# A two-layer attention trunk on one core: layer A's second projection moved ahead of the compression

## The chip, the cores and the metric

The kernel runs on one core of one Trainium2 chip. The metric is the device time of one execution in microseconds (us), taken as the median of several runs. The engines are named as in the profile: PE is TensorE (matmuls, and transposes done as matmuls), DVE is VectorE, ACT is ScalarE, POOL is GpSimd and SP is SyncE, which here only starts transfers.

## The reference

The input is one sequence of 512 rows of 1024 values, and a memory of 256 rows. Layer A normalizes the rows, projects them once, and runs two attentions beside each other; their outputs go through one output projection and are added to the input. An MLP with squared ReLU follows. Then keys and values are computed once for layer B, whose attention, output projection and second MLP end the program. All is in 32-bit floats.

Layer A's main attention has 12 heads in three groups of four, each group with its own keys and values. Each head attends three ways: to compressed blocks of 32 rows, to the selected blocks (with 512 rows, all 8 blocks are among the 16 that may be selected), and to a sliding window of 512 rows. Cut to what matters:

```python
k_c = rope(rmsnorm(compress(split_heads(k_cmp, G), 0), k_norm[0]), cmp_end)
v_c = compress(split_heads(v_cmp, G), 1)
...
def compress(t, i):
    tb = (t[:, :, blk_tok] + cmp_pos[i]).reshape(B, G, n_cmp, CMP_BLOCK * D)
    return jax.nn.gelu(tb @ cmp_w1[i] + cmp_b1[i]) @ cmp_w2[i] + cmp_b2[i]
```

The three results are weighted by sigmoid gates and summed. The memory attention has four heads over the 256 memory rows.

## The kernel before, in words

Every product of two 32-bit matrices is made of three matmuls on PE (mm3, lines 250 to 255): each operand is split into a high and a low part, and high by high, high by low and low by high are summed. Weights come in by SP's queue (L241), ACT makes their high part (L246), and DVE or POOL the low one (L248). Rows are handled in four blocks of 128.

Layer A is written as generators, which yield after a few instructions, and a few drivers that decide who goes next. Its opening, at L733 to L765, goes so:

- proj_a(0) projects group 0: four queries' heads, the keys of the selected and window branch, and the values. In each of the four blocks, evac takes the sums from PSUM: ACT copies the values (L899), normf computes the norms (L493 to L508), DVE scales by the norm weights (L903, L904), rope rotates (L517 to L520), L700 scales by the norm, hilo splits (L659, L660), and later PE transposes the queries (L709) and the keys (L719), which ACT (L715, L666, L667) and DVE (L665) copy out. Rotation and L700 run on POOL, but for group 0's even blocks, which use DVE.
- Woven with it is a second projection, of w_a0: the raw keys and values for the compression and the gates, 420 columns wide, whose four blocks stay in four buffers of tag x.
- Then a queue of filler work is built (Work). First in it is the compression: hidden(0) and hidden(1) transpose the raw rows (L797), copy them into three buffers of tag x each (L803, L804), add positions on POOL (L817), split (L288, L291) and multiply by w_c1; finish makes the compressed keys and values. mem_kv(0), the memory's keys and values of layer A, is woven into it; its memory tiles are split at L269 (ACT) and L270 (DVE). Behind it stand proj_a(1), proj_a(2), mem_q, mem_keys, mem_kv(1) (the memory's keys and values for layer B) and the first half of the output projection, outpart(0, 4).

Then attend (L142) walks through the attention items: 16 of each of the three groups, with 4 for the compressed blocks among them, and 8 of the memory attention. An item's front computes scores (L996 and L997 for the first two row blocks, L1009 and L1010 for the others), the maximum (L1000, L1012), the exponential on ACT (L216) and the scaling of the probabilities on POOL (L684). Its back transposes them (L1039, L1045), evT copies them out on DVE or ACT (L690, L692), and PE multiplies by the values (L1058). The memory items have L619, L638 and L646 for these. After each front and each back, attend takes some steps from the queue, 2.0 a time in group 0, 1.16 in group 1, 1.46 in group 2 and 1.96 in the memory items. An item whose group isn't projected yet makes the queue run up to that name ("g1", "g2", "cmp", "mem").

That is the order in which the program is written. A scheduler then places the instructions of each engine with a simulated timeline, so the order on an engine differs from that of the source. Pools set limits on top: PSUM has 2 accumulator tiles (acc), 3 for scores (ps), 2 for transposes (pt) and 1 for outputs (po); in SBUF tag x has 8 buffers, the weights' tag w 4, and the rotated rows' tags tq and qki 2 each.

Of the kernel before, what the change touches and what calls it, by code (L numbers as in the profile page):

```python
# [68 lines left out]
def drain(*gens):  # L69
    for g in gens:  # L70
        for _ in g:
            pass


def chain(*gens):
    for g in gens:
        yield from g


def weave(main, fill, ratio):  # L80

    due, fill = 0.0, iter(fill)
    for _ in main:
        due += ratio
        while due >= 1.0:
            due -= 1.0
            if next(fill, END) is END:
                due = -1e9
        yield
    yield from fill  # L90
# [43 lines left out]
def paced(gen, n):  # L134

    while True:
        for _ in range(n):
            yield
        next(gen, None)
# [33 lines left out]
def spread(a, b, at, every):  # L173

    a = list(a)
    for i, x in enumerate(b):
        a.insert(at + i * (every + 1), x)
    return a


class K:
    def __init__(self, ctx, tc, ins, out):
# [12 lines left out]
        self.lab = "s"  # L195

    BUFS = dict(
        act=12, st=3, w=4, qk=8, pt4=4, p2=6, raw=2, tmp=4, sq=1, rb=1, tq=2, qki=2, ki=2, x=8, r1=1, r2=1, r3=1, r4=2, r5=2, r6=3, r7=2, nm=6, su=5, cr=6, c1=2, c2=2, nb=4,
        cs=2, stt=4, vcb=1, ab=1,
    )  # L200

# [523 lines left out]
    def layer_a(self):  # L725
        nc, ins = self.nc, self.ins
        xg = self.xg0
        ab = self.t("ab", [P, 768])
        gt = ab[:, 0:144].rearrange("p (b g) -> p b g", b=NB)
        KC = self.c("KC", [P, 3, 2, 32], F32R)  # L730
        vc = ab[0:96, 144:208]
        raw0, st = [], []

        def evac0(b, ps):
            t = self.t("x", [P, 420])
            nc.scalar.activation(t, ps, AF.Copy, scale=st[0][:, b : b + 1])
            raw0.append(t)
            ga = gt[:, b, :]
            nc.vector.tensor_scalar(out=ga, in0=t[:, 384:420], scalar1=-1.0, scalar2=80.0, op0=ALU.mult, op1=ALU.min)
            nc.scalar.activation(ga, ga, AF.Exp)  # L740
            nc.vector.tensor_scalar(out=ga, in0=ga, scalar1=1.0, scalar2=None, op0=ALU.add)
            nc.vector.reciprocal(out=ga, in_=ga)

        ga, kf, qm, kk, oT, om = [[] for _ in range(3)], [], [], [], [], []
        x0 = self.x

        def hook(k):
            if k + 1 < KT:
                self.xpart(k + 1)
            i = self.square(k, x0[k], nc.vector)  # L750
            if k == KT // 2:
                self.constants_in(i)
            if k == KT - 1:
                self.setup2()
                st.extend(self.stats_cols())
                self.ms = self.mem_stats()

        self.xpart(0)
        p0 = self.proj_a(
            0, xg, st, ga[0], banks=[self.pacc] * 2 + [self.pS] * 2, lo="v", fine=True, hook=hook  # L760
        )
        for _ in range(KT):
            next(p0)
        drain(weave(p0, self.proj(xg, ins["w_a0"], 420, evac0, lo="g", pool=[self.pS, self.pacc, self.pacc, self.pS]), RC[0]))
        e = st[1]  # L765
        hidden, finish = self.compress(raw0, KC, vc)
        cmp = dict(KC=KC, vc=vc)
        work, seen, self.kf1 = Work(), [], []
        comp = chain(hidden(0, self.pacc), weave(hidden(1, self.pacc), finish(0), RC[1]), finish(1))
        work.add(weave(comp, chain(self.mem_kv(0, kf)), RC[2]), "cmp")  # L770
        work.add(self.proj_a(1, xg, st, ga[1]), "g1")
        work.add(self.proj_a(2, xg, st, ga[2]), "g2", lambda: seen.count(0) == 20)
        work.add(self.mem_q(0, xg, ins["w_am"], e, qm), None, lambda: seen.count(1) == 20)
        work.add(self.mem_keys(0, kf, kk), "mem")
        work.add(self.mem_kv(1, self.kf1))
        work.add(self.outpart(oT, 0, 4, ins["w_ao"], ins["xT"], 0))
        L, C = zip(*[self.attn_a(g, ga[g], gt, cmp, oT) for g in range(3)])
        M = self.mem_items(kf, qm, kk, om, 3, "mem")
        items = spread(L[0], C[0], 8, 0) + spread(L[1], C[1], 1, 1) + spread(L[2], C[2], 1, 1) + M
        slow = Work()  # L780
        slow.add(paced(self.adds, PA), None, lambda: len(seen) >= 12)
        attend(items, work, slow, RA, seen)
        while work.step() is not END:
            pass
        drain(self.outpart(oT + om, 4, 8, ins["w_ao"], None, 4))
# [978 lines left out]
```

## Time and profile before

| | |
|---|---|
| median of 3 runs | 1319.93 us |
| the runs | 1315.16, 1319.93, 1320.21 us |
| span of the profiled execution | 1316.2 us |
| PE busy | 1266.8 us |
| DVE busy | 860.7 us |
| ACT busy | 772.2 us |
| POOL busy | 377.6 us |

The page lists for the profiled execution its span, from the first instruction to the last; its own time with what lies around the span is not listed apart. The span stands 3.7 us below the median of the runs, and 1.0 above the fastest of them. Layer A's attention ends about 353 us after the span's start; MLPs and layer B take the rest. Busy times overlap: the sum over the engines is far above the span.

### The profile page before, as it was taken

How to read it: one execution, taken by the hardware profiler on the slowest of the kernel's cores; microseconds unless marked ns; L12 is line 12 of the kernel's file. 1: busy time of each engine (PE TensorE's matmuls, PEld its weight loads, DVE VectorE, ACT ScalarE, POOL GpSimd, SP SyncE). 2: the span in 40 equal slices, each digit the busy share in tenths (PEclk: the TensorE clock that was granted, in tenths of full speed). 3: DMA queues.
4: the chain of work that ended last, by engine and by line, in shares of the span. 5: the costliest groups of instructions: out<-in, count | busy, mean ns of one | idle time of the engine just before them, and what ended most of it. 6: DMA issues, size and time to landing. Idle time of an engine off the chain costs nothing.

```text
span 1316.2 us, 18557 instructions
## 1 busy us (share of the span) xinstructions
PE 1266.8 (96%) x6468; PEld 1041.7 (79%) x6468; DVE 860.7 (65%) x1597; ACT 772.2 (59%) x1699; POOL 377.6 (29%) x478
## 2 busy tenths in 40 slices
PE   9789989999999999999999989989999999999998
PEld 7768777677688888888887888877768888888887
DVE  6987767744566656566588566675665655747566
ACT  6765668674575354453557457777657545354462
POOL 4455574443240000000003679562324000000000
PEclk9899989999999999999999999999999999999999
DMA  7333222334379697796965431210338879697434
GB/s 263 120 98 106 97 97 81 63 74 113 120 245 240 219 279 219 262 247 208 290 197 165 134 79 49 67 45 9 95 120 267 232 269 225 221 280 223 154 112 160
DMA packets 61837, 215.28 MB, mean 164 GB/s; under 512 B 6736, under 2 KB 14928, under 8 KB 61232
## 3 DMA queue, kind: packets, MB, share of 16 engines
q1 hardware_dynamic: 50800, 143.72, 32.9%
q0 software_dynamic: 9344, 35.77, 13.8%
q10 hardware_dynamic: 1600, 34.61, 7.2%
q8 instruction: 51, 0.84, 0.2%
q14 instruction: 42, 0.34, 0.1%
HBM read 208.83 MB, written 72.35 MB: 214 GB/s over the span
## 4 chain that ended last, share of the span: by engine, by line
PE 81%; DVE 8%; ACT 4%; issue 2%; POOL 2%; DMA 2%; POOLq 0%; ACTq 0%; DVEq 0%
PE s_ps L253 13%; PE s_ps L254 13%; PE s_ps L255 13%; PE s_acc L253 6%; PE s_acc L254 6%; PE s_acc L255 6%; PE s_pt L253 3%; PE s_pt L254 3%; PE s_pt L255 3%; PE s_po L1058 2%; DVE s_w L248 2%; PE s_ps L1500 1%; PE s_pt L1045 1%; ACT s_p L216 1%; PE s_ps L1009 1%
## 5 line engine op out<-in xcount | busy, mean ns | idle before, releaser
L248 DVE TENSOR_TENSOR s_w<-s_st,s_w 128x1024 fp32r<-128x1024 f32 (+3 forms) x240 | 290.1, 1213 | 260.3 <-ACT s_w L246 259.8
L246 ACT ACTIVATE s_w<-s_st 128x1024 fp32r<-128x1024 f32 (+4 forms) x272 | 263.8, 973 | 188.0 <-PE s_pt L255 49.5
L253 PE MATMUL s_ps<-s_act,s_w 128*128 128x512 f32 x568 | 222.6, 394 | 1.4 <-ACT s_act L288 1.4
L254 PE MATMUL s_ps<-s_act,s_w 128*128 128x512 f32 x568 | 222.0, 391 | 0.0
L255 PE MATMUL s_ps<-s_act,s_w 128*128 128x512 f32 x568 | 221.8, 391 | 0.0
L253 PEld LDWEIGHTS s_ps<-s_act,s_w 128*128 128x128 f32 x568 | 106.8, 188 | 26.1 <-ACT s_act L288 3.1
L254 PEld LDWEIGHTS s_ps<-s_act,s_w 128*128 128x128 f32 x568 | 106.9, 188 | 22.9 <-issue 0.8
L255 PEld LDWEIGHTS s_ps<-s_act,s_w 128*128 128x128 f32 x568 | 106.9, 188 | 22.1
L253 PE MATMUL s_acc<-s_w,s_act 128*128 128x512 f32 (+3 forms) x288 | 103.8, 365 | 4.5 <-DVE s_tq L1424 2.6
L254 PE MATMUL s_acc<-s_w,s_act 128*128 128x512 f32 (+3 forms) x288 | 103.4, 361 | 2.2 <-DVE s_w L248 1.4
L216 ACT ACTIVATE s_p<-s_ps 128x512 f32<-128x512 f32 x64 | 38.2, 597 | 112.6 <-PE s_ps L255 112.6
L255 PE MATMUL s_acc<-s_w,s_act 128*128 128x512 f32 (+3 forms) x288 | 101.5, 358 | 0.0
L1128 POOL DMA_DIRECT2D sum<-in_w_db_dram x16 | 14.4, 902 | 300.0 <-ACT s_p L216 298.3
L684 POOL TENSOR_SCALAR s_p<-s_p,s_cr 128x256 f32<-128x256 f32 (+3 forms) x128 | 71.6, 581 | 73.3 <-DVE s_cr L1021 21.7
L216 ACT ACTIVATE s_p<-s_ps,s_nm 128x256 f32<-128x256 f32 (+3 forms) x128 | 65.6, 522 | 17.6 <-DVE s_nm L1000 7.5
L248 POOL TENSOR_TENSOR s_w<-s_st,s_w 128x512 fp32r<-128x512 f32 (+4 forms) x32 | 52.2, 1630 | 59.3 <-ACT s_w L246 59.2
L253 PEld LDWEIGHTS s_acc<-s_w,s_act 128*128 128x128 f32 x288 | 56.5, 196 | 12.5 <-DVE s_tq L1424 3.0
L692 ACT ACTIVATE s_pt<-s_pt 128x512 f32<-128x512 f32 (+2 forms) x97 | 50.7, 529 | 25.2 <-PE s_pt L638 12.1
L254 PEld LDWEIGHTS s_acc<-s_w,s_act 128*128 128x128 f32 x288 | 56.5, 196 | 7.3 <-DVE s_w L248 2.2
L255 PEld LDWEIGHTS s_acc<-s_w,s_act 128*128 128x128 f32 x288 | 56.3, 196 | 4.8 <-issue 0.6
L288 ACT ACTIVATE s_qk<-s_p 128x256 fp32r<-128x256 f32 (+1 forms) x96 | 46.9, 489 | 22.0 <-DVE s_p L1138 20.1
L1128 POOL DMA_DIRECT2D sum<-sum x16 | 14.1, 884 | 143.5 <-issue 45.8
(338 smaller groups left out, 2995.2 us busy)
## 6 DMA issues: line engine op xcount, KB each, us to landing
s_st<-in_w_up_dram SPq DMA_DIRECT2D x64, 512.0 KB, 4.3
s_st<-sum SPq DMA_DIRECT2D x64, 512.0 KB, 6.0
s_st<-in_w_db_dram SPq DMA_DIRECT2D x48, 512.0 KB, 4.3
sum<-in_w_db_dram POOLq DMA_DIRECT2D x16, 1024.0 KB, 13.5
sum<-sum POOLq DMA_DIRECT2D x16, 1024.0 KB, 9.8
s_st<-in_w_bq_dram SPq DMA_DIRECT2D x16, 384.0 KB, 3.2
s_st<-in_w_ag_dram SPq DMA_DIRECT2D x11, 512.0 KB, 4.5
s_st<-in_w_c_dram SPq DMA_DIRECT2D x8, 512.0 KB, 3.7
```

Source lines behind the costliest of these rows:

```text
L216: return lambda *a, **k: self.marks.append(f(*a, **k))
L246: nc.scalar.activation(w[:, 0], st, AF.Copy)
L248: e.tensor_tensor(out=w[:, 1], in0=st, in1=w[:, 0], op=ALU.subtract)
L253: mm(ps, lh[0], rh[0], start=start, stop=False, skip_group_check=again)
L254: mm(ps, lh[0], rh[1], start=False, stop=False, skip_group_check=again)
L255: mm(ps, lh[1], rh[0], start=False, stop=stop, skip_group_check=again)
L288: nc.scalar.activation(dst[:, 0], src, AF.Copy)
L684: self.nc.gpsimd.tensor_scalar(out=p, in0=p, scalar1=c, scalar2=1.0, op0=ALU.mult, op1=ALU.mult)
L692: self.nc.scalar.activation(dst, src, AF.Copy)
L1009: nc.tensor.matmul(Sp, q[:, blk], kk[hl][:, br, 0:n], start=hl == 0, stop=False)
L1058: nc.tensor.matmul(O[x * 64 : x * 64 + 64, q0 + o : q0 + 256], v[:, j, br, :], st[x][br][:, j, o:256], start=half == 0 and br == 0 and j = ...
L1128: self.behind(self.nc.gpsimd.dma_start(t[o], x, accum_op=ALU.add, max_dma_last_dim=4096))
```

## The change

The second group's projection is run to its end before compress is set up, and mem_kv(1) takes its place in the queue. Since group 1 is done by then, its name is entered as done. One more buffer of tag x holds group 1's values, and the scratch for descriptors of transfers that POOL issues is set to 8192 bytes, where no size was given before. After the added line, the numbers of the lines below are higher by one.

```diff
     BUFS = dict(
-        ... x=8, ...
+        ... x=9, ...
...
         drain(weave(p0, self.proj(xg, ins["w_a0"], 420, evac0, lo="g", pool=[self.pS, self.pacc, self.pacc, self.pS]), RC[0]))
         e = st[1]
+        drain(self.proj_a(1, xg, st, ga[1]))
         hidden, finish = self.compress(raw0, KC, vc)
...
         work.add(weave(comp, chain(self.mem_kv(0, kf)), RC[2]), "cmp")
-        work.add(self.proj_a(1, xg, st, ga[1]), "g1")
+        work.add(self.mem_kv(1, self.kf1))
+        work.done.add("g1")
         work.add(self.proj_a(2, xg, st, ga[2]), "g2", lambda: seen.count(0) == 20)
         work.add(self.mem_q(0, xg, ins["w_am"], e, qm), None, lambda: seen.count(1) == 20)
         work.add(self.mem_keys(0, kf, kk), "mem")
-        work.add(self.mem_kv(1, self.kf1))
         work.add(self.outpart(oT, 0, 4, ins["w_ao"], ins["xT"], 0))
...
-    nc = bacc.Bacc("TRN2", target_bir_lowering=False, num_devices=1)
+    nc = bacc.Bacc("TRN2", target_bir_lowering=False, num_devices=1, dynamic_dma_scratch_size=8192)
```

What that does to the order of each engine shows at three places. The first is PE at the end of the opening's projections, before the change. The rows show line, instruction, the tile written and the tiles read; s_pt is a tile for transposes, s_qki holds split rows, s_ps are scores (here of group 0).

```order
L709 MATMUL s_pt_495<-idr,s_qki_467 128x128 x4
L719 MATMUL s_pt_502<-idr,s_qki_467 128x128 x2
L996 MATMUL s_ps_663<-s_qk_124,s_qk_122 128x256
L996 MATMUL s_ps_663<-s_qk_125,s_qk_122 128x256
L997 MATMUL s_ps_663<-cm,idr 128x256
L996 MATMUL s_ps_721<-s_qk_124,s_qk_122 128x512
L996 MATMUL s_ps_828<-s_qk_124,s_qk_122 128x256
L996 MATMUL s_ps_828<-s_qk_125,s_qk_122 128x256
L997 MATMUL s_ps_828<-cm,idr 128x256
L709 MATMUL s_pt_554<-idr,s_qki_529 128x128 x4
```

The same place after the change; acc_676 and acc_736 are accumulators of group 1's first two blocks.

```order
L255 MATMUL s_ps_631<-s_w_424,s_act_256 128x420
L997 MATMUL s_ps_936<-s_qk_124,s_qk_122 128x256
L997 MATMUL s_ps_936<-s_qk_125,s_qk_122 128x256
L998 MATMUL s_ps_936<-cm,idr 128x256
L709 MATMUL s_pt_554<-idr,s_qki_529 128x128 x4
L997 MATMUL s_ps_994<-s_qk_124,s_qk_122 128x512
L253 MATMUL s_acc_676<-s_w_668,s_act_119 128x512
L253 MATMUL s_acc_736<-s_w_668,s_act_119 128x512
L719 MATMUL s_pt_561<-idr,s_qki_529 128x128 x2
L997 MATMUL s_ps_994<-s_qk_125,s_qk_122 128x512
```

Scores follow scores before; now group 1's 96 matmuls begin between them. They end 111 rows further down. The second block's transposes (s_pt_495) have moved up into the projection, and the first block's (s_pt_433) stand 18 matmuls earlier than before.

The second place is POOL behind group 0's last rotation, before the change: s_p are probabilities, s_tmp the rows of the compression.

```order
L700 TENSOR_TENSOR s_tq_579<-s_tq_579,s_r_109_576 128x384
L684 TENSOR_SCALAR s_p_121_669<-s_p_121_669,s_cr_672 128x128 x2
L684 TENSOR_SCALAR s_p_137_727<-s_p_137_727,s_cr_730 128x256 x2
L684 TENSOR_SCALAR s_p_163_834<-s_p_163_834,s_cr_837 128x128 x2
L684 TENSOR_SCALAR s_p_178_917<-s_p_178_917,s_cr_920 128x256 x2
L817 TENSOR_TENSOR s_tmp_746<-s_x_677,c_115 128x4x31
L817 TENSOR_TENSOR s_tmp_790<-s_x_677,c_115 128x4x31
```

After the change the additions for the compression stand behind four rotations; the last of them reads so, with s_tq_910 the rows of group 1's fourth block.

```order
L700 TENSOR_TENSOR s_tq_848<-s_tq_848,s_r_155_845 128x384
L517 TENSOR_TENSOR s_rb_913<-s_tq_910,c_115 128x384
L518 TENSOR_TENSOR s_tq_910<-s_tq_910,c_115 128x384
L519 TENSOR_TENSOR s_tq_910<-s_tq_910,s_rb_913 128x6x32
L520 TENSOR_TENSOR s_tq_910<-s_tq_910,s_rb_913 128x6x32
L684 TENSOR_SCALAR s_p_258_1302<-s_p_258_1302,s_cr_1306 128x384
L684 TENSOR_SCALAR s_p_259_1303<-s_p_259_1303,s_cr_1306 128x384
L700 TENSOR_TENSOR s_tq_910<-s_tq_910,s_r_165_907 128x384
L818 TENSOR_TENSOR s_tmp_1019<-s_x_950,c_115 128x4x31
L818 TENSOR_TENSOR s_tmp_1063<-s_x_950,c_115 128x4x31
```

Four groups of L517 to L520 and L700, for s_tq_724, 786, 848 and 910, have moved ahead of the twelve additions (L818 after the change); before, they stood behind them, spread among the probabilities of group 0's later items.

The third place is PE where group 0 hands over to group 1, before the change. s_pt_1821 is group 1's last transposes, s_po_1812 group 0's output, s_ps_1914 scores of group 0.

```order
L709 MATMUL s_pt_1821<-idr,s_qki_1781 128x128 x4
L1009 MATMUL s_ps_1914<-s_qk_124,s_qk_123 128x512
L1058 MATMUL s_po_1812<-s_pt_391_1755,s_x_369 64x256
L1058 MATMUL s_po_1812<-s_pt_373_1676,s_x_369 64x128
L1058 MATMUL s_po_1812<-s_pt_391_1755,s_x_369 64x128
L1058 MATMUL s_po_1812<-s_pt_373_1676,s_x_369 64x256
L1058 MATMUL s_po_1812<-s_pt_391_1755,s_x_369 64x256
L1058 MATMUL s_po_1812<-s_pt_373_1676,s_x_369 64x128
L1058 MATMUL s_po_1812<-s_pt_391_1755,s_x_369 64x128
L719 MATMUL s_pt_1828<-idr,s_qki_1781 128x128 x2
L1009 MATMUL s_ps_1914<-s_qk_125,s_qk_123 128x512
L1010 MATMUL s_ps_1914<-cm,idr 128x128
```

After the change:

```order
L997 MATMUL s_ps_2216<-s_qk_664,s_qk_662 128x512
L997 MATMUL s_ps_2216<-s_qk_665,s_qk_662 128x512
L998 MATMUL s_ps_2216<-cm,idr 128x2x128
L930 MATMUL s_ps_2240<-KC,s_qk_662 128x64 x2
L930 MATMUL s_ps_2240<-KC,s_qk_663 128x64 x2
L997 MATMUL s_ps_2273<-s_qk_664,s_qk_662 128x256
L997 MATMUL s_ps_2273<-s_qk_665,s_qk_662 128x256
L998 MATMUL s_ps_2273<-cm,idr 128x256
L254 MATMUL s_acc_2530<-s_w_2114,s_act_256 128x512
L255 MATMUL s_acc_2530<-s_w_2114,s_act_256 128x512
L253 MATMUL s_acc_2922<-s_w_2914,s_act_119 128x256
```

No transposes of group 1 stand here any more: scores of group 1 (s_ps_2216, s_ps_2273) run among the last matmuls of group 2's projection (acc_2530), and the memory queries (acc_2922) begin behind them.

More of the change, by code (lines that the diff above doesn't have):

```diff
@@ L197 @@
     BUFS = dict(
-        act=12, st=3, w=4, qk=8, pt4=4, p2=6, raw=2, tmp=4, sq=1, rb=1, tq=2, qki=2, ki=2, x=8, r1=1, r2=1, r3=1, r4=2, r5=2, r6=3, r7=2, nm=6, su=5, cr=6, c1=2, c2=2, nb=4,
+        act=12, st=3, w=4, qk=8, pt4=4, p2=6, raw=2, tmp=4, sq=1, rb=1, tq=2, qki=2, ki=2, x=9, r1=1, r2=1, r3=1, r4=2, r5=2, r6=3, r7=2, nm=6, su=5, cr=6, c1=2, c2=2, nb=4,
         cs=2, stt=4, vcb=1, ab=1,
```

## The prediction, on record before the run

> **What bounds the kernel now.** I read the page first: how busy each engine is over the span, what clock TensorE was granted, and who owns the chain that ended last.
>
> ```profile
> span 1316.2 us, 18557 instructions
> PE 1266.8 (96%) x6468; PEld 1041.7 (79%) x6468; DVE 860.7 (65%) x1597; ACT 772.2 (59%) x1699; POOL 377.6 (29%) x478
> PEclk9899989999999999999999999999999999999999
> PE 81%; DVE 8%; ACT 4%; issue 2%; POOL 2%; DMA 2%; POOLq 0%; ACTq 0%; DVEq 0%
> ```
>
> TensorE (PE) is the bound: busy 96%, 81% of the chain. The change takes no matmul away and adds none, so it can pay in two coins only: idle time of PE, and stretches in which the granted clock is below 9 tenths. Both lie in the first quarter, in layer A. So the next view is PE's timeline there. Columns: start, length, instruction, and in brackets the idle time before it with its releaser.
>
> ```profile
> 39.65 0.35 PE L254 MATMUL s_acc<-s_w,s_act 128*128 128x420 f32 x1
> 43.84 0.35 PE L255 MATMUL s_acc<-s_w,s_act 128*128 128x420 f32 x1
> 46.53 0.66 PE L709 MATMUL s_pt<-idr,s_qki 128*128 128x128 f32 x4 [2.34 <-DVE s_qki L660]
> 48.42 0.55 PE L253 MATMUL s_ps<-s_w,s_act 128*128 128x420 f32 x1
> 48.77 0.55 PE L254 MATMUL s_ps<-s_w,s_act 128*128 128x420 f32 x1
> 53.69 0.47 PE L996 MATMUL s_ps<-s_qk,s_qk 128*128 128x256 f32 x2
> 57.97 1.19 PE L996 MATMUL s_ps<-s_qk,s_qk 128*128 128x512 f32 x3 [3.69 <-DVE s_qk L665]
> 63.34 1.12 PE L797 MATMUL s_pt<-c,s_x 128*128 128x128 f32 x4 [0.28 <-ACT s_qk L715]
> 73.89 1.01 PE L797 MATMUL s_pt<-c,s_x 128*128 128x128 f32 x4 [2.65 <-DVE s_pt L690]
> 77.28 0.44 PE L253 MATMUL s_acc<-s_w,s_qki 128*96 128x256 f32 x1
> 77.91 0.40 PE L254 MATMUL s_acc<-s_w,s_act 128*128 128x512 f32 x1
> 78.15 0.39 PE L255 MATMUL s_acc<-s_w,s_act 128*128 128x512 f32 x1
> 181.88 1.17 PE L1045 MATMUL s_pt<-c,s_p 128*128 128x128 f32 x7 [1.38 <-ACT s_qk L667]
> 184.49 0.58 PE L253 MATMUL s_acc<-s_w,s_act 128*128 128x256 f32 x1 [1.45 <-DVE s_tq L904]
> ```
>
> Three things. The matmuls are pipelined, so one costs its pitch (start to start): between 39.65 and 43.84 lie 22 of them, 0.19 us each; a 128x512 one costs 0.233 (77.91 to 78.15). Behind the wait of 2.34 us the pitch is 0.35 (48.42 to 48.77): waits are paid for twice, once idle and once in clock. And the opening has no cover: 3.69 us at the first score of group 0 and 2.65 at the compression's transposes, while the first hidden matmul comes at 77.28, my milestone. By 181.88 PE waits for transposed keys and rotated rows of group 1. The stretches by window (busy time of PE, PEld, DVE, ACT, POOL, then PE clock, DMA share, GB/s):
>
> ```profile
> 185.00:190.00 5.00, 5.00 (x26) 5.00 (x24) 0.88 (x5) 2.06 (x7) 2.65 (x4) 0.50 0.73 260
> 212.00:278.00 66.00, 61.57 (x434) 46.32 (x432) 44.42 (x137) 50.83 (x166) 34.40 (x60) 1.00 0.33 74
> 300.00:340.00 40.00, 40.00 (x215) 29.73 (x214) 17.40 (x34) 16.71 (x48) 12.95 (x20) 1.00 0.40 112
> 400.00:500.00 100.00, 100.00 (x442) 82.78 (x442) 58.77 (x88) 52.75 (x78) 5.27 (x6) 1.00 0.83 241
> ```
>
> **The change, part by part.** *Opening before the first score.* In the old order mem_kv(0)'s conversions stand on ACT and DVE inside the evacuation of group 0.
>
> ```profile
> 33.49 1.72 ACT L269 ACTIVATE s_act<-s_st,gv 128x256 fp32r<-128x256 f32 x4
> 33.80 2.26 DVE L518 TENSOR_TENSOR s_tq<-s_tq,c 128x384 f32<-128x384 f32 x1
> 39.23 3.53 DVE L270 SCALAR_TENSOR_TENSOR s_act<-s_st,gv,s_act 128x256 fp32r<-128x256 f32 x4
> 42.68 0.56 DVE L506 SCALAR_TENSOR_TENSOR s_r<-s_r,ec,s_r 128x6 f32<-128x6 f32 x1
> 45.93 0.54 DVE L660 TENSOR_TENSOR s_qki<-s_tq,s_qki 128x384 fp32r<-128x384 f32 x1
> 49.23 0.54 DVE L518 TENSOR_TENSOR s_tq<-s_tq,c 128x384 f32<-128x384 f32 x1
> 33.45 2.19 POOL L248 TENSOR_TENSOR s_w<-s_st,s_w 128x840 fp32r<-128x840 f32 x1 [2.71 <-ACT s_w L246]
> ```
>
> They move behind group 1's weights. The 3.53 us just ahead of L506 go, and with them about 4 us of the path to the first transpose: its operand is ready near 42.5 instead of 46.5. PE gets there sooner too, since 18 matmuls (18 x 0.19 = 3.4) now follow it: at 40.6, so it still waits 1.9. Then 0.7 of transposes, 42 matmuls (8.0), 0.5 of transposes, and some of the slow clock: first score at about 52.1 instead of 53.69, 1.6 earlier (0 to 3). This is no term of its own: it goes into the next one.
>
> *Group 1 in the opening.* Its 96 matmuls, 96 x 0.233 = 22.4 us, now run where PE waited 3.69, among group 0's last transposes and first scores (about 5.9 by the rows at 46.53, 53.69 and 57.97 at full clock). Group 1's last block is accumulated at 52.1 + 28.3 = 80.4. Then comes a leg with little to cover it. All four blocks are rotated and scaled by POOL, in a row:
>
> ```profile
> 120.60 1.01 POOL L517 TENSOR_TENSOR s_rb<-s_tq,c 128x384 f32<-128x384 f32 x1 [8.54 <-DVE s_tq L904]
> 124.95 0.88 POOL L700 TENSOR_TENSOR s_tq<-s_tq,s_r 128x384 f32<-128x384 f32 x1
> 175.76 1.01 POOL L517 TENSOR_TENSOR s_rb<-s_tq,c 128x384 f32<-128x384 f32 x1
> 184.51 0.83 POOL L700 TENSOR_TENSOR s_tq<-s_tq,s_r 128x384 f32<-128x384 f32 x1
> 68.04 4.99 POOL L817 TENSOR_TENSOR s_tmp<-s_x,c 128x124 f32<-128x124 f32 x12
> ```
>
> A block takes 124.95 + 0.88 - 120.60 = 5.2 us alone and 184.51 + 0.83 - 175.76 = 9.6 in company. With probability scaling between them I take 6.1 each. The first two blocks share both accumulators and finish together, about halfway: 66. So POOL is through at 66 + 4 x 6.1 = 90.4, split included. PE has scores and transposes for some 5.6 of these 10 us and idles 4.4 at the last block's transposes. The compression's transposes stand behind them on PE; their copies, the 12 POOL additions (4.99) and the split bring the first hidden matmul 8.1 us later, at 98.5. (Before, that leg took 77.28 - 63.34 = 13.9, with attention's copies between.) Less group 1's own PE time, 22.4 plus 1.9 of transposes, 98.5 - 24.3 = 74.2 stands against 77.28: **-3.1**. With a block at 5.2 or 9.6 the ends are -6.7 (4 x 0.9 = 3.6 less, when PE's own work ends as late as POOL's) and +10.9 (14.0 more); nearer the first, since the four blocks meet only two weight splits.
>
> Waits here touch the clock as well: 2.34 us of idle at 46.53 were enough to halve it, as were 1.38 + 1.45 at 181.88. I count 0.4 for the 1.9 us left at the first transposes, and nothing behind the 4.4 us, since POOL and not PE is late in the 8.1 us that follow. [...]
>
> *Hand-off from group 0 to group 1.* Rows 181.88 and 184.49 cost 1.38 + 1.45 idle, and the half clock behind them (0.50 from 185 to 190, about 6.8 us in all) costs half of its length, 3.4. Both waits are for group 1's last blocks, which are now done 90 us earlier: **-6.2** (0, should the next group's memory queries wait in like manner, to -6.2).
>
> *Cover given away and won.* Filler is conserved; its place is not. Before, 206 rows of PE's order (the 212 to 278 window) ran without filler, and PE idled 66 - 61.57 = 4.4, 7%. Now that window holds the output projection's first half, and bare are about 40 rows in group 0's second half, 113 rows at the end of group 2 and the memory items' start, and 45 in their tail with 27 matmuls: 200 rows, so at this price nothing changes. But the tail was fully covered (300 to 340: 40.00 of 40), and a memory item leans on ACT:
>
> ```profile
> L216 ACT ACTIVATE s_p<-s_ps,s_nm 128x256 f32<-128x256 f32 x40 | 18.8, 480 | 8.4 <-DVE s_nm L1000 6.1 <-PE s_pt L1045 1.8 <-DVE s_nm L675 0.5
> L216 ACT ACTIVATION_READ_ACCUMULATOR s_p<-s_ps,s_nm 128x1 f32 x112 | 23.8, 212 | 0.0
> L692 ACT ACTIVATE s_pt<-s_pt 128x512 f32<-128x512 f32 x33 | 20.1, 608 | 10.5 <-PE s_pt L1045 5.2 <-PE s_pt L638 4.3 <-PE s_pt L1039 0.8
> L246 ACT ACTIVATE s_w<-s_st 128x512 fp32r<-128x512 f32 x16 | 10.0, 630 | 21.2 <-DMA s_st<-in_w_ao_dram 19.6 <-PE s_ps L255 1.6
> ```
>
> Two exponentials and a copy, 2 x (0.48 + 0.21) + 0.61 = 2.0 us an item, plus 8 weight conversions of 0.63 = 5.0 for eight items. If those 5.0 all show, +5; half is +2.5. Group 0's bare part follows right behind a half of the filler that it had; I add 1 for it, an estimate by 7% of some 14 us: **+3.5** (-1 to +6).
>
> *Scratch and ninth row buffer.* [...]
>
> ```profile
> sum<-in_w_db_dram POOLq DMA_DIRECT2D x16, 1024.0 KB, 13.5
> ```
>
> There POOL is busy 5.27 of 100 us and PE 100.00: **0**. Were a landing of 13.5 exposed once, it would be +13.5. The ninth buffer only lets group 1's values live beside group 0's, the four raw rows and the three of the compression; I count it at nothing.
>
> Sum: -3.1 - 6.2 + 3.5 = -5.8 us on the profiled execution. Its span of 1316.2 lies 3.7 below the median of the runs, 1319.93; the difference carries over, 1319.93 - 5.8 = **1314.1**. A measurement of this kernel can tell about 0.5%, 6.6 us, from no change.
>
> **Rivals.** *A, the gaps close and nothing is given back:* a block in 5.2, the hand-off gone, the cover at its better end: -6.7 - 6.2 - 1 = -13.9, **1306.0**. For it: 200 bare rows against 206; against it: ACT in the memory items.
>
> *B, slower: POOL's row of four blocks.* If they run at 9.6 as at 175.76, POOL is through at 66 + 38.4 = 104.4, 14 us later, and everything on PE behind the last transposes, the compression above all, waits: -5.8 + 14.0 = +8.2, **1328.1**. It decides from -5.8 + 4(b - 6.1) = 0, b = 7.6 us a block; at 9.2 the kernel is over 0.5% slower. For it: DVE's L518 took 2.26 beside POOL's L248 and 0.54 without; both engines are at their densest here. [...] Against it: at 120.60 a block ran in 5.2 in the middle of attention.
>
> *C, a shuffle:* the waits reappear at the next dependence, with the same sum; **1320**.
>
> **How the numbers follow.** Forecast 0.45, A 0.22, B 0.21, C 0.12. Of the forecast's share, with the hand-off uncertain upwards and the block's length both ways (its own range 1309 to 1320), 0.13 lies beyond 0.5% faster, 0.02 slower. Faster: 0.13 + 0.22 + 0.02 of C = 0.37. Slower: 0.02 + 0.18 of B + 0.02 of C = 0.22. The rest, 0.41, is within 0.5%. The range runs from a little below A, 1304, to just above B, 1329.
>
> **What would show it.** Right: first score near 52; no wait above 1 us at the hand-off from group 0 to 1, clock 1.0 there; group 1's POOL blocks at 5 to 6.5 us; first hidden matmul at 95 to 101; a wait of 3 to 6 us at the last group-1 transposes. Wrong: blocks above 7.6 us (B), PE idle above 5 us in the memory items' tail, or a first hidden matmul beyond 105. And if layer B or an MLP moves by over 3 us, my zero for the scratch is wrong.

## The result, and the profile after

The change makes the kernel slower by 1.0%. Median after 1329.56 us (1324.56 to 1332.34, 6 runs), before 1317.65 us (1313.27 to 1320.21, 6 runs); ratio 1.0101, interval 1.0077 to 1.0124. Forecast was 1314.1, 0.44% faster than the median then shown, with a range up to 1329. The profiled execution of the changed kernel took 1326.93 us with a span of 1325.2, 9.0 more than before. The page after:

```profile
span 1325.2 us, 18572 instructions
PE 1263.9 (95%) x6468; PEld 1041.0 (79%) x6468; DVE 860.3 (65%) x1601; ACT 771.5 (58%) x1695; POOL 373.7 (28%) x478
PEclk9979899999999999999999999999899999999999
PE 77%; DVE 8%; DMA 6%; ACT 5%; issue 3%; POOL 2%; ACTq 0%; POOLq 0%; DVEq 0%
```

No engine has more work than before, and PE as many matmuls. What changed is where PE waits: the third slice (about 66 to 99 us) went down to a clock of 7 tenths, and PE's share of the last chain from 81% to 77%, while that of DMA rose from 2% to 6%. The loss is all in layer A. Its end, the first matmul of the output projection behind the last memory output, lies at 349.59 before and 361.13 after: 11.5 later. What follows takes 966.6 us before and 964.1 after.

Stretches of layer A, each cut at that kernel's own milestones (columns: busy time of PE, PEld, DVE, ACT, POOL, then PE clock, DMA share, GB/s), after:

```profile
80.00:90.00 10.00, 3.89 (x21) 3.06 (x19) 9.97 (x15) 8.15 (x21) 8.08 (x8) 0.75 0.45 154
90.00:100.00 10.00, 3.92 (x20) 3.10 (x20) 4.84 (x12) 4.52 (x11) 4.51 (x9) 0.50 0.16 52
106.00:153.00 47.00, 37.47 (x213) 31.16 (x211) 36.38 (x63) 28.26 (x59) 20.74 (x31) 0.93 0.42 130
180.00:190.00 10.00, 10.00 (x51) 8.02 (x50) 7.50 (x17) 6.58 (x20) 8.66 (x13) 1.00 0.30 107
225.00:361.00 136.00, 126.40 (x787) 95.86 (x787) 72.34 (x210) 81.10 (x247) 54.13 (x94) 0.97 0.34 82
```

And before, from its first hidden matmul to its last compressed values, and from 225 to the end of layer A:

```profile
77.00:120.00 43.00, 39.54 (x243) 33.90 (x242) 35.50 (x70) 26.21 (x54) 17.58 (x29) 0.99 0.50 155
225.00:350.00 125.00, 119.43 (x706) 87.36 (x705) 66.60 (x181) 75.88 (x225) 48.12 (x79) 1.00 0.37 95
```

The reading: length less busy time times clock is what PE lost. The compression's stretch loses 47.00 - 37.47 x 0.93 = 12.2 after and 43.00 - 39.54 x 0.99 = 3.9 before; the end of the layer 136.00 - 126.40 x 0.97 = 13.4 after and 125.00 - 119.43 = 5.6 before. The hand-off at 180 to 190 lost nothing after (PE 10.00 at 1.00), as forecast. For all kernels below I made the same sum in windows of 1 us, which weighs the clock where PE was busy. **The ledger** has that loss in us, with the time of each milestone. It is of one execution per kernel, and the total difference that it shows, 14.7, overstates the 11.5 by 3. One kernel below (the scratch alone) has the same order on every engine as the kernel before; its columns differ from the first row by up to 1.3 us, so differences of that size mean nothing.

```
kernel   start to first    to last com-     to 225   225 to end    total
         hidden matmul     pressed values            of layer A
before   18.4  ( 77.28)     3.6  (120.18)     8.7     5.3 (349.59)   36.1
after    23.6  (106.08)    12.3  (153.19)     2.1    12.9 (361.13)   50.8
```

PE's timeline after, at the places of which the prediction spoke (start, length, instruction, idle time before it with its releaser):

```profile
43.77 0.58 PE L709 MATMUL s_pt<-idr,s_qki 128*128 128x128 f32 x4 [2.77 <-DVE s_qki L660]
...
54.47 0.40 PE L997 MATMUL s_ps<-s_qk,s_qk 128*128 128x256 f32 x2
...
80.16 0.39 PE L255 MATMUL s_acc<-s_w,s_act 128*128 128x512 f32 x1
...
87.25 1.01 PE L1010 MATMUL s_ps<-s_qk,s_qk 128*128 128x384 f32 x2 [3.42 <-ACT s_p L216]
...
90.46 0.72 PE L709 MATMUL s_pt<-idr,s_qki 128*128 128x128 f32 x4 [2.10 <-DVE s_cr L1021]
...
94.74 0.72 PE L709 MATMUL s_pt<-idr,s_qki 128*128 128x128 f32 x4 [3.30 <-DVE s_qki L660]
...
100.11 1.84 PE L1040 MATMUL s_pt<-c,s_p 128*128 128x128 f32 x6 [1.94 <-issue]
...
106.08 0.31 PE L253 MATMUL s_acc<-s_w,s_qki 128*96 128x256 f32 x1
...
130.32 0.24 PE L253 MATMUL s_pt<-s_tmp,s_tmp 128*96 128x64 f32 x1 [2.15 <-DVE s_tmp L290]
...
143.34 0.36 PE L255 MATMUL s_acc<-s_w,s_qki 128*96 128x256 f32 x1 [1.22 <-DVE s_qki L291]
...
152.83 0.36 PE L851 MATMUL s_pt<-c,s_raw 96*128 96x96 f32 x2 [1.45 <-DVE s_raw L846]
...
293.39 0.80 PE L253 MATMUL s_acc<-s_act,s_w 128*128 128x512 f32 x1 [2.56 <-ACT s_w L246]
...
324.08 1.09 PE L1040 MATMUL s_pt<-c,s_p 128*128 128x128 f32 x4 [2.03 <-DVE s_pt L690]
```

Three groups of waits. The opening ends as forecast, but by two errors that cancel: the first score comes 2.4 late (54.47 for 52.1), and the way from there to group 1's last accumulation takes 26.1 us for 28.3, so that it ends at 80.55 for 80.4. Then, between group 1 and the compression, there are four waits of 1.9 to 3.4 us where the forecast had one of 4.4, and from 90 to 100 the clock is 0.50. Then come waits that it had not at all: in the compression (130 to 153, three shown), and at the layer's end (293.39, 324.08).

POOL's timeline after, for the four blocks of group 1 that stand in a row:

```profile
68.12 1.02 POOL L517 TENSOR_TENSOR s_rb<-s_tq,c 128x384 f32<-128x384 f32 x1 [2.10 <-DVE s_tq L905]
...
86.97 1.00 POOL L517 TENSOR_TENSOR s_rb<-s_tq,c 128x384 f32<-128x384 f32 x1 [1.44 <-DVE s_tq L905]
...
92.61 0.83 POOL L700 TENSOR_TENSOR s_tq<-s_tq,s_r 128x384 f32<-128x384 f32 x1
```

They take 92.61 + 0.83 - 68.12 = 25.3 us, 6.3 a block. Rival B needed over 7.6.

### The profile page after: what moved, and what is told of

Its sections match the earlier page's. It is cut to its first block, busy times and chain, and to the rows that moved or that the text cites. A ratio compares the mean times of both kernels' runs of the same rounds, so it can differ in the third digit from the quotient of the medians.

```text
span 1325.2 us, 18572 instructions
## 1 busy us (share of the span) xinstructions
PE 1263.9 (95%) x6468; PEld 1041.0 (79%) x6468; DVE 860.3 (65%) x1601; ACT 771.5 (58%) x1695; POOL 373.7 (28%) x478
## 3 DMA queue, kind: packets, MB, share of 16 engines
q0 software_dynamic: 9344, 35.77, 13.7%
## 4 chain that ended last, share of the span: by engine, by line
PE 77%; DVE 8%; DMA 6%; ACT 5%; issue 3%; POOL 2%; ACTq 0%; POOLq 0%; DVEq 0%
PE s_ps L254 13%; PE s_ps L255 13%; PE s_ps L253 13%; PE s_acc L253 5%; PE s_acc L254 5%; PE s_acc L255 5%; PE s_pt L255 3%; PE s_pt L254 3%; PE s_pt L253 3%; PE s_po L1059 2%; DVE s_w L248 2%; DMA s_st<-in_w_ao_dram 2%; ACT s_w L246 1%; ACT s_p L216 1%; PE s_ps L1501 1%
## 5 line engine op out<-in xcount | busy, mean ns | idle before, releaser
L692 ACT ACTIVATE s_pt<-s_pt 128x512 f32<-128x512 f32 (+2 forms) x93 | 48.0, 526 | 22.5 <-PE s_pt L1040 6.7
L288 ACT ACTIVATE s_qk<-s_p 128x256 fp32r<-128x256 f32 (+1 forms) x96 | 46.9, 489 | 22.1 <-DVE s_p L1139 20.1
## 6 DMA issues: line engine op xcount, KB each, us to landing
sum<-in_w_db_dram POOLq DMA_DIRECT2D x16, 1024.0 KB, 13.7
```

The costliest lines, as they stand in the source:

```text
L288: nc.scalar.activation(dst[:, 0], src, AF.Copy)
L692: self.nc.scalar.activation(dst, src, AF.Copy)
```

## The experiments

Every kernel was timed in five rounds beside the kernel before on its chip; ratios are to that, since the kernel before itself took between 1310.9 and 1317.65 us from one session to the next. One number of the ledger recurs: the loss **behind the first hidden matmul** (the second to fourth columns together), 17.6 before and 27.3 after.

**Layer B's memory keys and values (mem_kv(1), "the memory keys" below) go back to their old place.** From the changed kernel:

```
-        work.add(self.mem_kv(1, self.kf1))
         work.done.add("g1")
...
         work.add(self.mem_keys(0, kf, kk), "mem")
+        work.add(self.mem_kv(1, self.kf1))
```

> The changed kernel with the memory's keys and values for layer B put back to their old place behind the memory keys; group 1 stays in the opening. Up to the compression's first half PE's order is that of the changed kernel; behind it PE's filler is group 2's projection, and from the start of group 1's attention on, the order is that of the kernel before. Theory (the changed kernel loses about 5 us at the boundary between group 1 and the compression, about 8 in the compression's second half because the memory projection brings its own conversions there, about 5.6 in the uncovered end of layer A, and wins 5 at the hand-off): the last two losses go, so about 1318 + 5 + 2 - 5 = 1320 us (1317 to 1324), first hidden matmul unchanged at 106. Rival (the compression's chain itself waits, whoever fills): 1326 to 1331.

Measured: 1318.66 against 1311.36, ratio 1.0055 (1.0036 to 1.0074). Windows of this kernel over the compression and over the layer's end:

```profile
106.00:152.00 46.00, 42.17 (x249) 36.20 (x248) 34.67 (x68) 26.19 (x54) 16.88 (x30) 0.96 0.45 145
225.00:352.00 127.00, 121.43 (x721) 89.38 (x720) 68.15 (x186) 77.20 (x231) 49.58 (x82) 1.00 0.37 94
```

The compression's loss falls from 12.3 to 5.5 in the ledger, the layer's end to 5.3 (127.00 - 121.43 = 5.6 by these rows), what it was before. The opening keeps its 23.8. So about half of the slowdown belongs to the place of mem_kv(1).

**Buffer and scratch alone; the scratch alone.** From the kernel before:

```
-        ... x=8, ...
+        ... x=9, ...
...
-    nc = bacc.Bacc("TRN2", target_bir_lowering=False, num_devices=1)
+    nc = bacc.Bacc("TRN2", target_bir_lowering=False, num_devices=1, dynamic_dma_scratch_size=8192)
```

> The kernel before with the ninth row buffer and the scratch of 8192 bytes alone. Theory: no cost, ratio 0.998 to 1.002. Rival (the smaller scratch delays transfers that POOL issues, in the MLPs or layer B): 5 us slower or more, with PE idle in the MLP.

> The kernel before with the scratch of 8192 bytes alone; the order of every engine is that of before. Theory A (the 0.28% that ninth buffer and scratch cost together come from the orders that the ninth buffer shifts, in the opening and in layer B's loads): ratio 0.998 to 1.0015. Theory B (the smaller scratch): ratio 1.002 to 1.004.

Measured: both together 1316.01 against 1311.36, 1.0028 (1.0012 to 1.0044); the scratch alone 1314.5 against 1314.69, 1.0005 (0.9986 to 1.0024). The scratch costs nothing that can be seen. So the 0.28% would be the ninth buffer's, but the two intervals overlap, and its profiled layer A doesn't show it: it ends at 347.59, earlier than before.

**The compression's raw rows ahead of group 1.** From the changed kernel:

```
+        hidden, finish = self.compress(raw0, KC, vc)
+        h0 = hidden(0, self.pacc)
+        for _ in range(2):
+            next(h0)
         drain(self.proj_a(1, xg, st, ga[1]))
-        hidden, finish = self.compress(raw0, KC, vc)
...
-        comp = chain(hidden(0, self.pacc), ...
+        comp = chain(h0, ...
```

> The changed kernel with the compression's first transposes and copies issued ahead of group 1's projection, everything else as changed. Theory (the new gap of 12 us idle at 82 to 106 is the compression's preparation, transposes, copies, 12 additions and split, queued behind group 1's last block): the first hidden matmul comes at about 96 instead of 106, 8 us faster than the changed kernel, about 1321 us (1318 to 1325). Rival (POOL's row of four rotations is what is late, whatever stands behind it): PE still waits for the last rotated block and the time falls by 3 or less.

Measured: 1328.36 against 1311.36, 1.0121 (1.0092 to 1.015). My theory fell: the first hidden matmul came at 104.00, 2 us earlier instead of 10. Rows of PE and of POOL in this kernel:

```profile
76.17 1.01 PE L1013 MATMUL s_ps<-s_qk,s_qk 128*128 128x384 f32 x2 [4.59 <-ACT s_p L216]
...
104.00 0.53 PE L253 MATMUL s_acc<-s_w,s_qki 128*96 128x256 f32 x1 [2.89 <-ACT s_qki L288]
```

```profile
78.45 1.01 POOL L517 TENSOR_TENSOR s_rb<-s_tq,c 128x384 f32<-128x384 f32 x1
...
102.15 0.83 POOL L700 TENSOR_TENSOR s_tq<-s_tq,s_r 128x384 f32<-128x384 f32 x1
```

With the twelve additions ahead of them, POOL's four blocks begin 10.3 us later (78.45 for 68.12) and end at 102.98, 6.1 each. The additions were through by 78.50, and still the first hidden matmul waited: the split that it needs (L288 on ACT) was not moved with them. It stands on ACT behind the split of group 1's last block, which POOL's last scaling holds up to 103.01, and comes at 103.44. Moving that split too was not tried.

**Half of group 1's rotations to DVE.** From the changed kernel:

```
-            en = nc.vector if g == 0 and b % 2 == 0 else nc.gpsimd
+            en = nc.vector if g < 2 and b % 2 == 0 else nc.gpsimd
```

> The changed kernel with the even two of group 1's four blocks rotated and scaled on DVE instead of POOL, as group 0 has it. Theory (all three engines queue at the boundary, and DVE is busy 9.97 of 10 us at 80 to 90): 0 to 3 us faster than the changed kernel, 1326.5 to 1329.5. Rival (POOL's row alone is late): POOL is through 10 us earlier and the time falls by 6 or more, below 1324.

Measured: 1326.18 against 1311.36, 1.0105 (1.0077 to 1.0133); first hidden matmul at 104.22. Taking work from POOL does little, which fits that DVE is as full there: 9.97 of 10 us from 80 to 90 in the windows of the kernel after.

**Group 1's rotation left out.** From the changed kernel:

```
-            self.rope(t, self.cs[:, b], en)
+            if g != 1:
+                self.rope(t, self.cs[:, b], en)
```

> The changed kernel without the rotation of group 1's rows (four POOL instructions a block, 3.4 us, left out; scaling, split and transposes stay). Theory (POOL's row of group 1's blocks, 68.1 to 93.4 us in the changed kernel, sets when the compression's preparation may start): the row ends near 84, the first hidden matmul comes at 97 to 100 instead of 106, and the time falls by 6 to 8 us, ratio about 1.005. Rival (the weight conversions for the compression and the memory, queued on ACT and DVE ahead of the last block's evacuation, are late): first hidden matmul after 103, 3 us or less, ratio 1.008 or more.

Measured: 1317.64 against 1314.69, 1.0019 (1.0001 to 1.0038); first hidden matmul at 100.77. POOL's last scaling of the row in this kernel:

```profile
87.79 0.83 POOL L700 TENSOR_TENSOR s_tq<-s_tq,s_r 128x384 f32<-128x384 f32 x1
```

It is through 4.8 us earlier than in the kernel after (92.61), and the first hidden matmul follows by 5.3. So rival B named a resource that is on the path; only its price was not the one that B gave it. The kernel does less work than the others, so the rest of its gain isn't read as an ordering effect.

**The three edits together** (keys back, raw rows first, half of the rotations on DVE).

```
+        h0 = hidden(0, self.pacc)
...
+            en = nc.vector if g < 2 and b % 2 == 0 else nc.gpsimd
...
         work.add(self.mem_keys(0, kf, kk), "mem")
+        work.add(self.mem_kv(1, self.kf1))
```

> The changed kernel with three edits: memory projection for layer B back at its old place, compression's first transposes and copies ahead of group 1, even blocks of group 1 rotated on DVE. Theory (raw rows first failed because its 12 additions pushed POOL's row of rotations back by 10 us; with half of the row gone both fit): first hidden matmul at 95 to 98, ratio to the kernel before 0.998 to 1.002. Rival (DVE takes up what POOL gives): first hidden matmul after 102, ratio 1.004 to 1.008.

Measured: 1324.26 against 1314.69, 1.008 (1.0054 to 1.0105), first hidden matmul at 101.92: within 0.1 us of what the rival had, and far from the theory. It is no better than the first edit alone, and these orders don't mend the opening.

**Layer A's memory keys and values (mem_kv(0)) as cover for the boundary.** From the changed kernel:

```
         drain(self.proj_a(1, xg, st, ga[1]))
+        drain(self.mem_kv(0, kf))
...
-        work.add(weave(comp, chain(self.mem_kv(0, kf)), RC[2]), "cmp")
+        work.add(comp, "cmp")
```

> The changed kernel with layer A's memory projection (48 matmuls, 11.2 us) run between group 1 and the compression instead of woven into the compression. Theory (the boundary is a gap without independent work): PE's idle time at 82 to 106 falls from 12 us to 3 or less, but the compression then stands bare, with 6 to 10 us more of waits behind, so that the time stays within 4 us of the changed kernel, ratio 1.007 to 1.013. Rival (cover at the boundary is all that is missing): 8 us or more faster, ratio below 1.004.

Measured: 1325.34 against 1314.69, 1.0082 (1.0054 to 1.0109). The loss up to the first hidden matmul falls from 23.6 to 16.0, and the compression's rises from 12.3 to 19.1, with a new wait on PE:

```profile
123.48 0.53 PE L253 MATMUL s_acc<-s_w,s_qki 128*96 128x256 f32 x1 [5.28 <-ACT s_qki L288]
```

Of the 7.6 us gained ahead of the compression, 6.8 are paid inside it.

**Group 1's values in a buffer of their own.** From the changed kernel, with x back at 8:

```
-                v.append(self.t("x", [P, NB, 2, HD]))
+                v.append(self.t("v1" if g == 1 else "x", [P, NB, 2, HD]))
```

> The changed kernel with group 1's values in a buffer of their own and 8 row buffers as before, so that layer B's loads stand in the old order. Theory (the ninth row buffer costs 0.28% by the orders that it shifts, scratch nothing): 2 to 5 us faster than the changed kernel, ratio 1.005 to 1.009, with layer A's end near 360 as before. Rival (those orders cost nothing beside the moved projection): ratio 1.009 to 1.013.

Measured: 1329.38 against 1310.9, 1.0135 (1.0116 to 1.0154). No gain; the theory that the ninth buffer's effect on the later order explains the rest fell.

**The memory keys moved, and nothing else.** From the kernel before:

```
+        work.add(self.mem_kv(1, self.kf1))
         work.add(self.proj_a(1, xg, st, ga[1]), "g1")
...
         work.add(self.mem_keys(0, kf, kk), "mem")
-        work.add(self.mem_kv(1, self.kf1))
```

> The kernel before with one edit: the memory projection for layer B stands ahead of group 1's projection in the queue; group 1 stays behind the compression. Theory (in the compression's tail this projection is poor filler, since it brings 16 splits of memory rows and four weight conversions for 48 matmuls, where group 1 brings four conversions for 96): waits of 4 to 8 us more at the compression's second half and ratio 1.003 to 1.007. Rival (any filler covers the tail; the changed kernel's second loss comes from the move of group 1 alone): ratio 0.998 to 1.002.

Measured: 1327.29 against 1310.9, ratio **1.0122** (1.0105 to 1.014). I had expected at most 1.007. One moved line costs as much as the whole change. Its windows over the compression and over the layer's end:

```profile
74.00:124.00 50.00, 42.54 (x236) 36.14 (x237) 40.12 (x70) 29.98 (x61) 24.59 (x34) 0.93 0.46 149
225.00:361.00 136.00, 126.51 (x800) 97.14 (x799) 72.04 (x199) 78.15 (x240) 55.44 (x93) 0.97 0.31 76
```

They are those of the kernel after, though group 1 isn't in the opening: a clock of 0.93 and 0.97, and 10.6 and 12.5 us lost in the ledger. The waits on PE are of the same kinds and at the same places, two of them here:

```profile
111.20 0.36 PE L255 MATMUL s_acc<-s_w,s_qki 128*96 128x256 f32 x1 [2.46 <-DVE s_qki L291]
...
291.88 0.50 PE L253 MATMUL s_acc<-s_act,s_w 128*128 128x512 f32 x1 [2.38 <-ACT s_w L246]
```

**Lighter memory keys.** From the changed kernel, mem_kv(1) without its low parts; the other places where it reads them use the high part twice:

```
+                    if l:
+                        nc.scalar.activation(a[:, 0, q, :], st[:, jj * 2 + q, :], AF.Copy, scale=g[:, k : k + 1])
+                    else:
+                        self.part(a[:, :, q, :], st[:, jj * 2 + q, :], g[:, k : k + 1])
...
```

> The changed kernel in which layer B's memory projection leaves out its low parts: 8 splits on DVE (L270) and 4 on DVE and POOL (L248) fall away, and PE uses the high part in their place, so that its matmuls stay the same in number and place; ACT's work and the loads stay. Theory (these splits, about 3.4 + 2.5 us of DVE and 4.8 of POOL, stand in the compression's second half in front of its own chain): PE's loss in idle time and slow clock between the first hidden matmul and the last compressed key falls from about 12 us to 8 or less, ratio 1.005 to 1.008. Rival (what costs is the place of the 48 matmuls alone: they are missing at the end of layer A, and group 1's 96 are missing here): ratio 1.009 to 1.012 and the loss at 106 to 155 us unchanged.

Measured: 1323.74 against 1314.49, 1.0083 (1.0058 to 1.0108). The compression's loss falls from 12.3 to 7.0, so 5.3 of its 8.7 us more than before go with those subtractions on DVE and POOL. The layer's end doesn't fall: 14.6 for 12.9. As a ratio it can't be told from the whole change, and this kernel too does less work than the others.

**Only group 1 in the opening**, the best of the parts: keys back, own buffer, x=8.

```
-        work.add(self.mem_kv(1, self.kf1))
         work.done.add("g1")
...
         work.add(self.mem_keys(0, kf, kk), "mem")
+        work.add(self.mem_kv(1, self.kf1))
...
+                v.append(self.t("v1" if g == 1 else "x", [P, NB, 2, HD]))
```

> The changed kernel with the memory projection for layer B at its old place and group 1's values in a buffer of their own, 8 row buffers as before. What is left is group 1 in the opening and the gap behind it. Theory: ratio 1.001 to 1.005, of which the boundary costs 5 us and the vanished hand-off gives back most. Rival (group 1 in the opening is a gain once the rest is put back): below 1.000.

Measured: 1317.04 against 1310.9, 1.0044 (1.0027 to 1.006). Its windows over the compression and the layer's end:

```profile
105.00:150.00 45.00, 41.12 (x249) 34.85 (x248) 34.34 (x66) 25.91 (x54) 17.71 (x29) 1.00 0.46 148
225.00:350.00 125.00, 119.46 (x707) 87.49 (x706) 66.90 (x182) 76.01 (x226) 47.65 (x80) 1.00 0.37 95
```

Both stretches are those of the kernel before again. This kernel differs from the one with the buffer of its own in the place of the memory keys alone, and both ran on one chip: 1317.04 for 1329.38, 12.3 us. No version tried beats the kernel before. The ledger of all of them:

```
                             to first   to com-    to    to end   behind first
                             hidden     pressed    225   of A     hidden
memory keys late
  before                      18.4        3.6      8.7     5.3        17.6
  buffer and scratch          16.7        5.1      6.3     4.9        16.3
  scratch                     18.8        4.9      7.4     5.4        17.7
  keys back                   23.8        5.5      4.4     5.3        15.2
  only group 1                23.0        3.9      4.5     5.3        13.7
  three together              23.5       10.2      6.4     5.5        22.1
memory keys early
  after                       23.6       12.3      2.1    12.9        27.3
  raw rows first              25.9       12.2      7.7     5.8        25.7
  half rotations on DVE       22.2       11.2      3.8    12.6        27.6
  rotation left out           19.0       11.4      3.5     8.2        23.1
  mem_kv(0) as cover          16.0       19.1      6.2     6.2        31.5
  own buffer                  22.5       11.9      5.4    14.7        32.0
  keys moved alone            14.1       10.6     12.9    12.5        36.0
  lighter keys                23.1        7.0      4.6    14.6        26.2
```

Whatever else was changed, early keys lose 23 to 36 us behind the first hidden matmul, late keys 14 to 22. The ranges all but touch; the three pairs that differ in the place of the keys alone are clear: 27.3 and 15.2 (after, keys back), 32.0 and 13.7 (own buffer, only group 1), 36.0 and 17.6 (keys moved alone, before).

## Why the prediction was wrong, step by step

**The cover, +3.5 (-1 to +6): the step that failed.** I counted the bare rows of PE (206 before, 200 after) and concluded that filler is conserved and its place nearly so. I didn't ask what each filler asks of the other engines. In the compression's tail group 1's projection was replaced by mem_kv(1), which converts its rows too: eight times L269 and L270 and four weights for 48 matmuls, where group 1 converted four weights for 96. The compression's own steps run on the same DVE. DVE after:

```profile
131.00 1.04 DVE L270 SCALAR_TENSOR_TENSOR s_act<-s_st,gv,s_act 128x256 fp32r<-128x256 f32 x2 [0.82 <-ACT s_act L269]
...
140.89 2.40 DVE L291 TENSOR_TENSOR s_qki<-s_tmp,s_qki 128x384 fp32r<-128x384 f32 x1 [1.40 <-ACT s_qki L288]
...
147.66 1.75 DVE L845 RECIPROCAL s_tmp<-s_tmp 96x256 f32<-96x256 f32 x1
149.64 2.71 DVE L270 SCALAR_TENSOR_TENSOR s_act<-s_st,gv,s_act 128x256 fp32r<-128x256 f32 x2 [0.23 <-ACT s_act L269]
152.27 0.41 DVE L846 TENSOR_TENSOR s_raw<-s_raw,s_tmp 96x256 f32<-96x256 f32 x1
```

The last rows show the mechanism. The compression's last product (L846) needs the reciprocal that is done at 149.41, and comes only at 152.27, because two conversions of the memory's rows stand ahead of it; PE waits 1.45 for it at 152.83. The two took 2.71 us, where two others took 1.04 at 131.00; POOL converted one of the same projection's weights beside them, from 149.29 to 151.67. The term measured +8.7 in the compression (12.3 - 3.6), a stretch that my sum didn't have at all, and +7.6 at the layer's end (12.9 - 5.3), where mem_kv(1) had been the cover: +16.3 for +3.5. That the early keys cause it is shown from both sides: taking them back removes it, moving them alone makes it. That their conversions do is shown for 5.3 of the 8.7 by the lighter keys.

At the layer's end I had priced ACT's conversions; the profile shows the loads ahead of them. With mem_kv(1) gone from there, the output projection's first half is the filler: 11 loads of its weights, 256 KB each, start from 280 to 335, for 8 before, and two of the large transfers that POOL issues fall into this stretch for one. Two of the loads stand in the last chain after, in order of time:

```profile
285.33 7.36 DMA s_st<-in_w_ao_dram
...
313.82 8.35 DMA s_st<-in_w_ao_dram
```

These are the two transfers of POOL, 1024 KB each, issued ahead of the two loads, and then DVE behind the second load:

```profile
283.02 0.95 POOL L1129 DMA_DIRECT2D sum<-in_w_db_dram  x1 [1.26 <-ACT s_p L216]
...
312.79 0.92 POOL L1129 DMA_DIRECT2D sum<-sum  x1
```

```profile
322.91 0.69 DVE L248 TENSOR_TENSOR s_w<-s_st,s_w 128x512 fp32r<-128x512 f32 x1 [2.73 <-ACT s_w L246]
323.52 0.41 DVE L690 COPY s_pt<-s_pt 128x256 f32<-128x256 f32 x1
```

The first load lands at 292.69, ACT converts it, and PE's wait ends at 293.39. At the second, DVE idles 2.73 us for the converted weight, and the attention's copy (L690) stands behind that in its order; PE, which waits for this copy, goes on at 324.08. So late filler held up the work that it was to cover. In the ledger's windows of 1 us, 290 to 300 and 320 to 330 lose 4.1 and 4.2 after, and 0.5 and 0.0 before: that is the +7.6 of the layer's end. Both loads ran beside POOL's transfers, which landed 9.3 and 9.6 us after their issue; the five loads from 299 to 324 that did not run beside them took 2.55 to 2.89 us. The longest load of these weights in layer A took 4.8 to 5.2 us in the six kernels with late keys, and 7.2 to 9.7 in the six with early keys that lose 8 us or more at the end; in the other two, raw rows first and mem_kv(0) as cover, it took 5.3 and 6.0, and they lose 5.8 and 6.2 there. This is read from the profiles: no run moves these transfers alone, and those two kernels lose more in other columns, 51.6 and 47.5 in all for 50.8.

**Boundary between group 1 and the compression, -3.1: wrong.** By the same milestone it is 106.08 - 24.3 - 77.28 = +4.5 (5.2 in the ledger). Its parts: POOL's row was right (6.3 a block for 6.1; done at 93.4 for 90.4, of which 2.1 is the later start, 68.1). Ahead of its last block I had not seen the evacuation's queue. ACT and DVE after:

```profile
83.44 0.37 ACT L900 ACTIVATE s_x<-s_acc,rc 128x128 f32<-128x128 f32 x1
```

```profile
86.29 0.41 DVE L904 TENSOR_TENSOR s_tq<-s_acc,gr 128x256 f32<-128x256 f32 x1
```

The accumulator is complete at 80.55, yet its copies come at 83.44 and 86.29, and POOL waits 1.44 for them. The last leg, from group 1's last transposes to the first hidden matmul, took 106.08 - 94.74 = 11.3 for 8.1, all but its last half microsecond at a clock of 0.50: I had put nothing down for the clock "since POOL and not PE is late". A first hidden matmul beyond 105 was one of my signs of being wrong. And PE idles not 4.4 us but about 12 between 80 and 100 (20 - 3.89 - 3.92 = 12.2 by the windows). The 3.69 and 2.65 us of waiting that group 1 was to fill weren't filled but moved behind it, which fits that its own evacuation and the compression's need the same engines. Two tries to fill the new gap (raw rows first, mem_kv(0)) paid elsewhere, and DVE in POOL's place brought 1.9 us up to the milestone (104.22 for 106.08).

**Hand-off, -6.2: right** in its mechanism, with no wait and a clock of 1.00 at 180 to 190. Its size is -6.6 in the ledger (8.7 to 2.1 up to 225). That it fits so closely may be luck: with the keys late the same column gives -4.3 and -4.2 (keys back, only group 1). **First score**, 52.1: 54.47, since the wait that was to shrink to 1.9 was 2.77 and the clock was 0.50 behind it, from 45 to 47. **Scratch, 0: right** (1.0005), though no run shows which transfers use it. **Ninth buffer, 0:** about right; 0.28% together with the scratch, not located, and no gain from doing without it (own buffer).

The sum by the ledger: +5.2 + 8.7 - 6.6 + 7.6 = +14.9 for -5.8; less the 3 by which it overstates, about the 11.5 by which layer A ends later.

Of the rivals, **A** has nothing left. **B** gives nearly the measured time (1328.1) by luck, for its cause wasn't there: its blocks of 9.6 measured 6.3. That POOL's row lies on the path is shown (rotation left out), but at the price that the forecast had already counted. **C**, waits that reappear at the next dependence, is what happened in kind, but not with the same sum.

**What stays open.** With the keys late, group 1 in the opening still costs 0.44 to 0.55% (the latter with the ninth buffer), while layer A ends where it did (349.72 for 349.59) in the one profile of it. The difference is below what two single executions can show.

## What to carry to other kernels

When work is moved as filler, count per matmul what it asks of the engines that convert and evacuate, and put that beside the queue of what it now runs with: here nearly equal rows on PE (200 bare for 206) weren't equal cover (+16.3 us for +3.5). Look at its loads as well: here two of them took 7.36 and 8.35 us, each beside a transfer four times as large, where five others took 2.55 to 2.89, and the conversions of these late weights held up PE (idle for 2.56 us) and the copy that stood behind one of them in DVE's order (DVE idle for 2.73). A gap in front of a chain of dependent steps on DVE, ACT and POOL was not filled here by a projection whose own evacuation needs the same three; it moved behind it. And of a change with several moved lines run each alone, the one that looks like mere housekeeping too: here that one was as dear as the whole.

## What the runs showed of the hardware

**The same wait, with and without the clock.** At 43.77 after, PE waited 2.77 us, and the clock from 40 to 50 was 0.83. With group 1's rotation left out, it waited 2.76 at the same place, at a clock of 1.00. PE's row and the window of that kernel, and behind them the window after:

```profile
43.30 0.53 PE L709 MATMUL s_pt<-idr,s_qki 128*128 128x128 f32 x4 [2.76 <-DVE s_qki L660]
```

```profile
40.00:50.00 10.00, 6.70 (x40) 5.88 (x38) 9.96 (x30) 6.10 (x19) 5.08 (x7) 1.00 0.00 0
```

```profile
40.00:50.00 10.00, 7.23 (x34) 6.68 (x33) 9.97 (x29) 5.66 (x18) 5.06 (x7) 0.83 0.00 0
```

The one lost 10 x 0.17 = 1.7 us by it, the other nothing. What makes the difference no profile here shows. Eight of the kernels above have a wait of 2.76 to 2.79 us at this place: by the clock in windows of 1 us it cost nothing in two of them (half of the rotations on DVE, rotation left out), 1.7 us in four, and 3.4 in two (raw rows first, three together). So the prediction's "waits are paid for twice" held in six of the eight. For a sum it means that such a wait had a clock price between 0 and 3.4 us here, which one profile doesn't tell.

**DVE beside POOL.** A subtraction of 128x384 (L291) took 2.40 us at 140.89, beside POOL's conversion of weights, and 0.55 in the compression before. POOL after, then DVE before:

```profile
140.48 2.39 POOL L248 TENSOR_TENSOR s_w<-s_st,s_w 128x1024 fp32r<-128x1024 f32 x1
```

```profile
107.14 0.55 DVE L291 TENSOR_TENSOR s_qki<-s_tmp,s_qki 128x384 fp32r<-128x384 f32 x1
```

The two instructions end within 0.42 us of each other. In the kernel with the lighter memory keys, in which POOL has no such conversion there, the last two subtractions of this shape in the compression took 0.54 and 0.56 (at 136.49 and 138.35). The prediction looked for a slowdown of this kind at POOL's blocks, which ran at 6.3 us; here it stands in the compression, where the moved filler brought two conversions to POOL (at 140.48 and 149.29).
